# Laying the PSUM slots of 512 columns ahead of those of 1024 at the seam between retention and attention in a hybrid decoder block

## The chip, the cores and the metric

The kernel runs on one core of one Trainium2 chip. The metric is the device time of one execution in microseconds (us). The profile and the trace come from one further execution under the hardware profiler. Engines are named as the profile names them: PE (TensorE matmul), PEld (its weight loads, which overlap PE), DVE (VectorE), ACT (ScalarE), POOL (GpSimd) and SP (SyncE, which here only issues transfers).

## The reference, cut to what matters

A decoder block on 1024 tokens of width 1024 in float32: a token mixer with two parallel branches, then a squared-ReLU MLP, each behind an RMS norm with modulation. The change sits where the first branch of the mixer (retention) ends and the second (dilated attention) begins.

```python
proj = h @ w_in
rq, rk, rv, rg = parts[0], parts[1], parts[2], parts[3]
ro = retention(rq, rk, heads(rv, RET_HEADS))          # 4 heads, chunks of 128 tokens
mu = jnp.mean(ro, axis=-1, keepdims=True)
var = jnp.mean(jnp.square(ro - mu), axis=-1, keepdims=True)
ro = (ro - mu) * lax.rsqrt(var + GN_EPS)              # per token and head
ret_out = (jax.nn.silu(rg) * (ro * gn_g + gn_b)) @ w_ret_out
...
for gi, (win, dil) in enumerate(ATT_GROUPS):          # 3 groups of 4 heads
    aq, ak, av = parts[4 + 3 * gi], parts[5 + 3 * gi], parts[6 + 3 * gi]
    o, lse = dilated_group(...)                       # scores, softmax, product with the values
...
merged = sigmoid(gate_a) * ret_out + sigmoid(gate_b) * att_out
```

## The kernel before

All products are made of three passes of PE with operands split into a high and a low part (`mm3`, lines 206 to 214: low weight, low operand, then high by high). Everything is written in one fixed order; each engine takes its instructions in that order, and waits on semaphores where a tile that it needs is not written yet, or where the tile it is about to overwrite is not yet read.

**The steps around the seam.** The retention runs as 32 steps, `chunk(h, c, ...)` for 4 heads of 8 chunks (line 717). In each, PE makes the chunk's output `o` (line 761 on). DVE takes its mean and variance (`bn`, `ba`, lines 777 to 779), POOL turns them into a scale and a shift (`gr`, lines 780 to 782), ACT applies them and so moves `o` out of PSUM into `onm` (line 790). The transposition of `onm` is left to the next step: `on_T` (line 675) has PE write four 128x128 transposes into a tile `oT` (line 682), and ACT copies them out (line 686). A step also spreads some products of the gate `rg` over its idle places (`rg_mm`); ACT reads those at line 709. The last chunk, number 31, has its `on_T` in the first step of the attention.

That step is `att_step(0, 0)` (line 1848). It makes `ak`, the projection that gives the keys of one head of group 1, as eight rounds (`proj_gen`) of six 128x512 matmuls: each round has two for each of the three passes, one per half of 1024 tokens. After four rounds stands `on_T` of the last chunk; then the other four. Behind them DVE multiplies the transposed outputs with the gate (`u_final`, line 693), POOL stores them to `y`, and ACT and DVE split `ak` into `kh` and `kl` (lines 1560 and 1561). The weights of this product are the tiles `raw_7785h` (ACT, line 200) and `raw_7785l` (DVE, line 201); those of the next product, which is the second step's `ak`, are `raw_7973h` and `raw_7973l`.

**PSUM.** It holds eight banks of 512 float32 columns per partition. A pool of PSUM slots is opened for each stage by `banks` (line 154) and closed by the next one. The tags take their banks in the order in which the stage first asks for them:

- retention, `banks(False, True)` at line 1438: a slot `s` is asked for first (line 1439), so that the 5 slots `s` of one bank are banks 0 to 4 and the 3 slots `rg` are banks 5 to 7;
- attention, `banks(False)` at line 1852: the 2 slots `mm` of two banks (`ps_mm`, 1024 columns) and the 4 slots `s` of one bank (`ps_s`, 512 columns); before, `ps_mm` asks first, at line 1853;
- retention's output product, `banks(True)` at line 2192: 8 slots `s`; its accumulators are `roc` (banks 4 to 1) and `roa` (banks 0, 7, 6 and 5, in this order).

A tile of a new pool waits until the tiles of the old pool that lay in its banks have been read. In the program before, the tiles lie so: the last chunk's `o` in bank 1, its predecessor's `oT` in bank 2; the first `ak` in banks 0 and 1, the second `ak` in banks 2 and 3, and the last chunk's `oT` in bank 4. Later, in the attention's output product `ao` (slots `mm`), the last two tiles lie in banks 0 and 1 and in banks 2 and 3; DVE reads them at line 2056.

**Transfers.** SP issues the loads of weights and spilled projections through a ring of three tiles (`raw`, line 85), each as soon as DVE is through with the tile's last use. The attention's bias comes at line 1529 (`bias`), spilled keys of group 2 at line 85 (`raw<-akd`). POOL issues the stores of `y` and, two per projection, sums in DRAM (`yt`, lines 575 and 577).

## Time and profile before

| what | us |
|---|---|
| median of 3 runs | 2169.19 |
| lowest and highest of them | 2168.49, 2170.26 |
| the profiled execution's own time | 2170.22 |
| its span in the profile | 2168.4 |
| PE busy in the span | 2143.3 (99%) |
| DVE, ACT, POOL busy | 1491.4, 983.1, 203.7 |

The profiled execution took 1.03 us more than the median of the runs, and its span is 1.82 us shorter than its own time. Times within the span are counted from its start. A row of the timeline gives start, duration, engine, line, operation, output and inputs, shape and count; in square brackets stands how long the engine was idle before, and what ended that idle time. A row of the waits gives the waiting instruction, what it waited for, the total in us, how often, and the longest. Matmuls overlap, so the distance between their starts (some 0.227 us at 512 columns) is shorter than the duration that a row shows (0.39 us).

### The profile page before, as it was taken

To read this page: it belongs to the slowest core of one execution; us is meant where nothing else is said; L and a number is where in the kernel's file an instruction comes from. 1 tells how busy PE (TensorE), PEld (TensorE's weight loads), DVE (VectorE), ACT (ScalarE), POOL (GpSimd) and SP (SyncE) were. 2 spreads that over 40 slices of the span, in tenths; PEclk is the share of its full clock that TensorE was granted. 3 is DMA by queue.
4 is the path that set the end of the run, shared out by engine and by line. 5 is a ranking of instruction groups with operands and counts; after the bars stand their busy time and mean duration, and the time that the engine had idled before them with its cause. 6 is when DMAs were issued, how large, how long until landed. Compare 5 with 4: busy or idle time off the path is not lost. (4 is left out here: it accounts for less than half of the span.)

```text
span 2168.4 us, 27396 instructions
## 1 busy us (share of the span) xinstructions
PE 2143.3 (99%) x10036; PEld 1784.0 (82%) x10036; DVE 1491.4 (69%) x2320; ACT 983.1 (45%) x1769; POOL 203.7 (9%) x267
## 2 busy tenths in 40 slices
PE   8999999999999999999999999999999999999998
PEld 6888888888888888888888888888778888888887
DVE  5886777777654677665667644677876665977855
ACT  5543322323344566664756635334454455533413
POOL 0001111100001243321010000001000000000003
PEclk9999999999999999999999999999999999999999
DMA  9859998845576655537877366653244435645322
GB/s 381 282 207 305 296 293 243 232 157 200 194 289 242 228 187 179 177 120 197 209 192 202 125 241 220 217 179 131 68 170 160 151 144 195 250 130 175 107 88 78
DMA packets 162931, 425.19 MB, mean 196 GB/s; under 512 B 28261, under 2 KB 56172, under 8 KB 159724
## 3 DMA queue, kind: packets, MB, share of 16 engines
q1 hardware_dynamic: 150456, 374.90, 49.0%
q0 software_dynamic: 9648, 48.24, 10.3%
q8 instruction: 79, 1.29, 0.2%
q10 hardware_dynamic: 2692, 0.30, 0.1%
q14 instruction: 56, 0.46, 0.1%
HBM read 324.13 MB, written 160.32 MB: 223 GB/s over the span
## 5 line engine op out<-in xcount | busy, mean ns | idle before, releaser
L212 PE MATMUL qap<-hl,qaw 128*128 128x512 f32 x264 | 102.7, 389 | 0.0
L214 PE MATMUL qap<-hh,qaw 128*128 128x512 f32 x264 | 102.7, 389 | 0.0
L210 PE MATMUL qap<-hh,qaw 128*128 128x512 f32 x264 | 102.7, 389 | 0.0
L620 POOL TENSOR_TENSOR j<-qk,j 128x512 fp32r<-128x512 f32 x32 | 42.8, 1336 | 399.6 <-ACT j L619 383.8
L2256 POOL TENSOR_TENSOR accnf<-accnf,sqnf 128x256 f32<-128x256 f32 (+1 forms) x18 | 16.6, 920 | 609.6 <-ACT sqnf L2252 609.6
L2360 ACT ACTIVATE a<-a 128x512 f32<-128x512 f32 x48 | 30.3, 632 | 73.7 <-DVE a L2359 73.7
L212 PEld LDWEIGHTS qap<-hl,qaw 128*128 128x128 f32 x264 | 49.6, 188 | 10.4
L210 PEld LDWEIGHTS qap<-hh,qaw 128*128 128x128 f32 x264 | 49.6, 188 | 10.3
L214 PEld LDWEIGHTS qap<-hh,qaw 128*128 128x128 f32 x264 | 49.5, 188 | 10.3
L2568 ACT CAST w2h<-w2s 128x512 fp32r<-128x512 f32 x36 | 22.4, 621 | 78.5 <-DVE w2s L2606 74.5
L686 ACT ACTIVATE on<-oT,gnt 128x128 f32<-128x128 f32 x128 | 48.1, 455 | 19.1 <-PE oT L682 18.9
L267 DVE TENSOR_TENSOR fw<-w1r,fw 128x512 fp32r<-128x512 f32 x48 | 32.8, 688 | 33.5 <-ACT fw L257 33.5
L267 DVE TENSOR_TENSOR qaw<-wa,qaw 128x512 fp32r<-128x512 f32 x66 | 44.0, 685 | 9.4 <-ACT qaw L257 9.4
L2091 DVE TENSOR_TENSOR rwl<-rwl,rwh 128x1024 fp32r<-128x1024 f32 x25 | 30.2, 1220 | 29.1 <-ACT rwh L2121 29.1
L210 PE MATMUL fp<-h2h,fw 128*128 128x512 f32 x128 | 50.0, 391 | 0.0
L214 PE MATMUL fp<-h2h,fw 128*128 128x512 f32 x128 | 49.8, 389 | 0.0
L212 PE MATMUL fp<-h2l,fw 128*128 128x512 f32 x128 | 49.8, 389 | 0.0
L214 PE MATMUL roa<-rh,rwh 128*128 128x512 f32 x128 | 49.8, 389 | 0.0
L210 PE MATMUL roa<-rh,rwl 128*128 128x512 f32 x128 | 49.8, 389 | 0.0
L212 PE MATMUL roa<-rl,rwh 128*128 128x512 f32 x128 | 49.8, 389 | 0.0
L1620 ACT ACTIVATE P<-P,ng 128x128 f32<-128x128 f32 (+1 forms) x96 | 41.9, 439 | 16.6 <-DVE ng L1612 16.5
L656 DVE TENSOR_TENSOR sm<-sm,sT 128x128 f32<-128x128 f32 x32 | 9.2, 288 | 54.7 <-ACT sm L655 54.7
(3092 smaller groups left out, 7216.8 us busy)
## 6 DMA issues: line engine op xcount, KB each, us to landing
v<-vd SPq DMA_DIRECT2D x32, 512.0 KB, 5.4
w1r<-in_w_ff_dram SPq DMA_DIRECT2D x32, 512.0 KB, 4.6
yt<-y POOLq DMA_DIRECT2D x24, 512.0 KB, 7.9
xsd<-as SPq DMA_DIRECT2D x24, 512.0 KB, 2.8
w2r<-in_w_ff2s_dram SPq DMA_DIRECT2D x24, 512.0 KB, 7.1
cossin<-in_w_ada_dram SPq DMA_DIRECT2D x22, 512.0 KB, 3.5
em<-in_w_ada_dram SPq DMA_DIRECT2D x16, 512.0 KB, 10.2
wrvs<-in_w_rv_dram POOLq DMA_DIRECT2D x16, 512.0 KB, 9.9
```

The costliest lines, as they stand in the source:

```text
L210: nc.tensor.matmul(o, wl, xh, start=first, stop=False, skip_group_check=skip)
L212: nc.tensor.matmul(o, wh, xl, start=False, stop=False, skip_group_check=skip)
L214: nc.tensor.matmul(o, wh, xh, start=False, stop=last, skip_group_check=skip)
L267: nc.vector.tensor_sub(t[:, 512:], src, fv(t[:, :512]))
L620: nc.gpsimd.tensor_sub(t[:, 1], src, fv(t[:, 0]))
L656: nc.vector.tensor_add(sm, sm, ps[:, C:2 * C])
L686: nc.scalar.activation(hd["on", h, c // 4][e][:, c % 4 * C:(c % 4 + 1) * C], po[:, e, :], AF.Identity, scale=gnv[0][:, neg + i:neg + i + 1 ...
L1620: nc.scalar.activation(v, v, AF.Exp, bias=ng[:, blk:blk + 1], accum_out=st[:, g, blk, 2 + a:3 + a])
L2091: nc.vector.tensor_sub(lo, fv(lo), fv(hi))
L2256: (nc.vector if f == 7 else nc.gpsimd).tensor_add(G["acc", key], G["acc", key], sq)
L2360: nc.scalar.activation(o, o, AF.Relu)
L2568: nc.scalar.copy(hi, src)
```

## The change

```diff
     def on_T(h, c):
 
-        po = ps_s(f"oT{h}{c}", (P, 4, P))
+        po = (hd.pop("oT", None) or ps_s(f"oT{h}{c}")).rearrange("p (a b) -> p a b", a=4)
         on = hd["o", h, c]
...
             if pair == a == 0:
                 banks(False)
+                hd["oT"] = ps_s("oT")
             ps = ps_mm(f"ak{pair}1{a}")
```

The tile for the last chunk's transposes is asked for ahead of the first `ak`, and `on_T` takes it when it comes. So the 4 slots `s` of the attention are banks 0 to 3, and its 2 slots `mm` banks 4 to 7. The other calls of `on_T` get the same tile as before, in another notation. Lines behind 1852 stand one further down in the changed file; line numbers in this document are those of before unless it says so. No instruction of any engine is added, dropped or moved; what changes is where PSUM tiles of the attention lie, and with it what the first users of a bank wait for. The first `ak` now lies in bank 4, where the `oT` of chunk 29 lay, and bank 5, where a tile of the last gate product but one lay; the second `ak` in banks 6 and 7, over the two tiles of the last gate product; the last `oT` in bank 0, over the `o` of chunk 30. The last `ao` tiles lie in banks 4 and 5 and in banks 6 and 7.

PE's order with its waits, at the first `ak` (`o_8465` is the last chunk's output, `oT_8475` the transposes of the chunk before it, `hh` and `hl` the normed input), before:

```order
L214 MATMUL o_8465<-v_8162,smh_8383 128x512
L682 MATMUL oT_8475<-ct,onm_8428 128x128 [waits Activation_49]
L682 MATMUL oT_8475<-ct,onm_8428 128x128 x3
L210 MATMUL ak_8501<-hh_86,raw_7785l 128x512 [waits Activation_49]
L210 MATMUL ak_8501<-hh_86,raw_7785l 128x512
L212 MATMUL ak_8501<-hl_94,raw_7785h 128x512 x2
```

and now:

```order
L214 MATMUL o_8465<-v_8162,smh_8383 128x512
L682 MATMUL oT_8475<-ct,onm_8428 128x128 [waits Activation_49]
L682 MATMUL oT_8475<-ct,onm_8428 128x128 x3
L210 MATMUL ak_8502<-hh_86,raw_7785l 128x512 [waits DVE_49]
L210 MATMUL ak_8502<-hh_86,raw_7785l 128x512
L212 MATMUL ak_8502<-hl_94,raw_7785h 128x512 [waits Activation_49]
```

The wait of before is for ACT's line 790 of the last chunk, which reads `o_8465` out of bank 1. Now the first matmul waits for DVE's line 201 that writes its own weight `raw_7785l`, and the third for ACT's line 200 that writes `raw_7785h`; nothing of the product waits for a reader of a bank any more.

Four rounds further on PE comes to the last chunk's transposes, `oT`, which now carry a wait of their own (rows of the changed program):

```order
L214 MATMUL ak_8502<-hh_89,raw_7785h 128x512 x2
L682 MATMUL oT<-ct,onm_8495 128x128 [waits Activation_49]
L682 MATMUL oT<-ct,onm_8495 128x128 x3
L210 MATMUL ak_8502<-hh_90,raw_7785l 128x512 x2
L212 MATMUL ak_8502<-hl_98,raw_7785h 128x512 x2
```

It is the wait for ACT's line 790 of the last chunk, whose result `onm_8495` they transpose; before, the product ahead of them had waited for the same instruction already, and they carried none. It has moved behind 24 matmuls.

The other place is PE's seam between the attention's output product and retention's, some 300 us later (`roa_11384` is the first accumulator there, in bank 0, `roa_11399` the second, in bank 7). The pieces of the difference:

```order
-L210 MATMUL roa_11384<-rh_11168,rwl_11118 128x512 [waits DVE_49,Activation_49]
+L210 MATMUL roa_11384<-rh_11168,rwl_11118 128x512 [waits Activation_49]
 L212 MATMUL roa_11384<-rl_11110,rwh_11244 128x512 [waits Activation_49]
 L214 MATMUL roa_11384<-rh_11168,rwh_11244 128x512
...
-L210 MATMUL roa_11399<-rh_11168,rwl_11118 128x512
+L210 MATMUL roa_11399<-rh_11168,rwl_11118 128x512 [waits DVE_49]
 L212 MATMUL roa_11399<-rl_11110,rwh_11244 128x512
 L214 MATMUL roa_11399<-rh_11168,rwh_11244 128x512
```

Before, the first accumulator waited for DVE's reading of the last `ao` tile but one, which had lain in bank 0. Now the second accumulator, 12 matmuls later, waits for DVE's reading of the very last `ao` tile, which had lain in banks 6 and 7. Otherwise one wait of PE on itself is gone from the second `ak` and one from the accumulator `roc` in bank 3; the orders of DVE, ACT, POOL and SP and their waits are the same as before.

## The prediction

> **What bounds the kernel.** I read the page first, then PE's waits, then the timeline around the changed place.

> ```profile
> span 2168.4 us, 27396 instructions
> PE 2143.3 (99%) x10036; PEld 1784.0 (82%) x10036; DVE 1491.4 (69%) x2320; ACT 983.1 (45%) x1769; POOL 203.7 (9%) x267
> ```

> PE is busy for 2143.3 of 2168.4 us, so at most 25.1 us can be won without taking work from it. What a change of waits is worth is read from the list of PE's own waits, here its first three rows:

> ```profile
> engine line waited for: us in total, times, longest us
> PE pb L444 <- DMA onehot<-in_onehot_dram: 5.6, 2, 4.3
> PE ak L210 <- ACT onm L790: 3.0, 1, 3.0
> PE fp L212 <- DVE xt L2398: 2.0, 2, 1.1
> ```

> The second row is the place of the change: once, the projection `ak` stood 3.0 us for ACT's line 790. No longer stall is in the list but the load at the start of the program. PE's timeline shows it from both sides:

> ```profile
> 974.06 0.60 PE L682 MATMUL oT<-ct,onm 128*128 128x128 f32 x4
> 977.69 0.73 PE L210 MATMUL ak<-hh,raw_7785l 128*128 128x512 f32 x2 [3.04 <-ACT onm L790]
> 978.26 0.62 PE L212 MATMUL ak<-hl,raw_7785h 128*128 128x512 f32 x2
> ...
> 983.28 0.60 PE L682 MATMUL oT<-ct,onm 128*128 128x128 f32 x4
> 983.63 0.71 PE L210 MATMUL ak<-hh,raw_7785l 128*128 128x512 f32 x2
> 984.18 0.62 PE L212 MATMUL ak<-hl,raw_7785h 128*128 128x512 f32 x2
> ```

> Both times four transposes stand ahead of the same kind of matmul. At 983.28 the product goes on 0.35 us after the first transpose began; at 974.06 it takes 3.63 us. Why, the other engines' rows between them show:

> ```profile
> 974.26 0.70 DVE L777 BATCH_NORM_STATS2 bn<-o 128x6 f32<-128x512 f32 x1 [3.74 <-PE o L214]
> ...
> 975.38 0.19 POOL L780 TENSOR_TENSOR gr<-ba,ct 128x1 f32<-128x1 f32 x1 [7.87 <-DVE ba L778]
> 975.64 0.92 POOL L781 TENSOR_TENSOR gr<-gr,ct 128x1 f32<-128x1 f32 x1
> 976.64 0.19 POOL L782 TENSOR_TENSOR gr<-gr 128x1 f32<-128x1 f32 x1
> 976.86 0.78 ACT L790 ACTIVATE onm<-o,gr 128x512 f32<-128x512 f32 x1 [0.67 <-POOL gr L782]
> ```

> The last chunk's `o` passes through DVE, POOL and ACT before ACT has read it out of bank 1, at 976.86 + 0.78 = 977.64; 0.05 us later PE starts `ak`, which lies in that bank. `ak` needs none of that chain's values: it is a wait for a place.

> **The change part by part.** No instruction is added or dropped, on any engine; what counts is which waits end last.

> (1) The wait for line 790 leaves the first `ak`. What takes its place are waits for the weights and, for the next product, the banks of the gate:

> ```profile
> 969.29 1.23 DVE L201 TENSOR_TENSOR raw_7785l<-raw,raw_7785h 128x1024 fp32r<-128x1024 f32 x1 [1.85 <-ACT raw_7785h L200]
> 971.98 1.08 ACT L709 ACTIVATE srg<-rg 128x512 f32<-128x512 f32 x2 [2.72 <-PE rg L214]
> ```

> The low weight is there at 970.52 and the high one, which it is made from, by 969.29, some 4 us ahead of need. The two tiles of the last gate product, under the second `ak`, are read by 973.06; the other two tiles under the first `ak` were read earlier. So PE goes on as it does at 983.28: 3.63 - 0.35 = 3.28 us won, and another 0.02 since the first two matmuls there are 0.55 us apart from the third, not 0.57. **3.30 us.** The bounds are the 3.04 us of recorded idle time below and 3.30 above; I take 3.30, since the row at 983.28 is the same sequence without the wait.

> (2) The last chunk's transposes now wait for line 790 themselves. They stand 5.59 us behind the start of `ak` (983.28 - 977.69), so they come at 983.28 - 3.30 = 979.98, and `onm` is there at 977.64: 2.34 us to spare, no cost. Were that cover gone, PE and all that is queued behind the transposes would wait by what is missing.

> (3) While `ak` now runs from 974.41, ACT and DVE still read `oT` and `o` from banks 2 and 1. The same overlap is in the trace: ACT's 1.50 us of copies out of `oT` beside `ak`,

> ```profile
> 983.91 1.50 ACT L686 ACTIVATE on<-oT,gnt 128x128 f32<-128x128 f32 x4 [5.34 <-PE oT L682]
> 984.40 4.30 DVE L693 TENSOR_TENSOR on<-on,srg 128x512 f32<-128x512 f32 x7 [3.97 <-ACT on L686]
> ```

> where `ak` keeps its pace (0.62 us for a pair, at 984.18 as at 978.26). Cost 0. These rows also show that the followers move along: ACT waits for the transposes, DVE for ACT; POOL's stores of `y` and SP's later loads wait for DVE. They come 3.30 us earlier with PE.

> (4) At the seam some 300 us later, the second accumulator `roa` now waits until DVE has read the last `ao`:

> ```profile
> 1282.69 0.39 PE L210 MATMUL roa<-rh,rwl 128*128 128x512 f32 x1
> ...
> 1282.89 1.22 DVE L2056 TENSOR_TENSOR g<-g,ao 128x1024 f32<-128x1024 f32 x1 [4.22 <-PE ao L214]
> ...
> 1285.41 0.39 PE L210 MATMUL roa<-rh,rwl 128*128 128x512 f32 x1
> ```

> The 13th matmul of `roa` starts at 1285.41, and the reading ends at 1282.89 + 1.22 = 1284.11. DVE was idle for 4.22 us before it, waiting for PE, so it keeps this distance: 1.30 us to spare, cost 0. If DVE were late by more than that, PE would wait for the excess, with ACT and DVE behind it; that needs a second thing to be late, and nothing in the change makes one. The wait that leaves the first `roa` cost nothing either: there is no row for it in PE's waits.

> The sum against the profiled execution: 3.30 us, so the span goes from 2168.4 to 2165.1 and its own time from 2170.22 to 2166.9. That execution stands 1.03 us over the median of the runs; for the median, 2169.19 - 3.30 = **2165.9 us**.

> **Does it last to the end?** Later waits of PE (such as the row with `fp`) are for DVE and ACT working on PE's own results, and move along. Only transfers could keep their old times. This is the place with the least room:

> ```profile
> 1003.13 1.01 ACT L1560 CAST kh<-ak 128x1024 fp32r<-128x1024 f32 x1 [10.82 <-PE ak L214]
> ...
> 1009.62 0.32 SPq L85 DMA_DIRECT2D raw<-akd  x1
> ...
> 1019.01 1.05 ACT L1551 CAST kh<-raw 128x1024 fp32r<-128x1024 f32 x1 [6.03 <-DMA raw<-akd]
> ...
> 1019.08 0.51 POOL L577 DMA_DIRECT2D yt<-yt  x1 [9.41 <-DMA yt<-y]
> ...
> 1020.10 1.23 DVE L1552 TENSOR_TENSOR kl<-raw,kh 128x1024 fp32r<-128x1024 f32 x1 [3.73 <-ACT kh L1551]
> ...
> 1022.21 0.28 PE L212 MATMUL sc<-kl,qh 128*128 128x128 f32 x1
> ```

> The keys of group 2 land 9.39 us after SP's issue, `kl` is ready at 1021.33, and PE wants it at 1022.21: 0.88 us to spare. The issue itself follows DVE's work behind `kh` at 1003.13, which waits for PE, so it moves along too.

> **The rivals.**

> A. Transfers keep their times. If those keys land at 1019.01 as before, `kl` is ready at 1021.33, where PE now wants it at 1022.21 - 3.30 = 1018.91: a new stall of 2.42 us, and 0.88 us is left of the gain: 2168.3. For it speaks that the load runs in a crowded stretch, as the window of its ten us shows:

> ```profile
> 1010.00:1020.00 10.00, 10.00 (x64) 8.88 (x63) 5.74 (x8) 3.97 (x10) 0.51 (x1) 1.00 0.86 240
> ```

> The last but one number is the mean busy share of the DMA engines, 0.86. Against it: `kh` at 1003.13 ended a wait of 10.82 us for PE, so the issue follows PE, and the transfers beside it follow the stores of `y`, which follow PE too. [...]

> B. Slower. The issue order at the same place changes: the earlier load falls behind one more whole `yt` transfer of POOL, 9.41 us by its row. It would be issued at 1006.32, land 18.80 us later at 1025.12, and `kl` be ready another 2.32 us on (1021.33 - 1019.01) at 1027.44: a stall of 8.53 us against 1018.91, net 5.23 us slower: 2174.4. It decides from a landing of 9.39 + 0.88 + 3.30 = 13.57 us after the issue. Against it: POOL's `yt` sums follow the stores of `y`, which move by the same 3.30 us, and one `yt` transfer already ran beside this load.

> C. The change does not remove the wait: PE starts `ak` at 977.69 for another reason. Then the time stays at 2169.2. Against it: nothing else that `ak` waits for ends after 970.52.

> **How the numbers follow.** Forecast 2165.9 with 0.84; A 0.07, B 0.05, C 0.04. A measurement of this kernel can tell from no change about 0.2%, which is 4.34 us: 3.30 us lies within it. The fastest run of before is 0.70 us under the median, the slowest 1.07 over, so the forecast may read 2164.8 to 2167.0, and a reading below 2164.85 has some 0.08, from the forecast's tail. Slower holds B's 0.05; the rest, 0.87, is within 0.2%. The range reaches from 2164.0 (the forecast less 1.07 for the scatter of the runs and 0.8, a quarter of the gain, for what I may have sized too small) to 2169.4 (A with 1.07 more, which takes in C); it leaves out B.

> **What would show it.** In the changed kernel's profile, PE's list has no row of `ak` on line 790, the first `ak` matmul stands 0.35 us behind the transposes (at 974.41), the last transposes follow 5.57 us later without idle time, and no row of `roa` on DVE's line of `ao` (one line further down now) appears. A shows as a new row of `sc` waiting for `kl`, with 2 us or so; B as the same row with more than 3.3. The prediction is wrong if the gain in the span is under 2 or over 4.3 us.

## The result, and the profile after

The changed kernel took 2165.70 us, the median of 22 runs (2164.59 to 2172.95). The kernel before, on the same chip, took 2170.15 us, also the median of 22 runs (2168.07 to 2175.38). The ratio is 0.9979, with a 95% interval of 0.9972 to 0.9985: 4.5 us won, and by the interval between 3.3 and 6.1 us. The predicted 2165.9 us is within 0.2 us of the measured time, but partly by luck. The gain was not the predicted 3.30 us but 1.2 us more, and the three runs that the prediction started from lay 1.0 us under the median of the 22.

The profiled execution of the changed kernel took 2165.45 us. Its span and engine totals:

```profile
span 2163.6 us, 27394 instructions
PE 2141.4 (99%) x10036; PEld 1782.8 (82%) x10036; DVE 1492.1 (69%) x2320; ACT 983.5 (45%) x1769; POOL 203.2 (9%) x267
```

The span is 4.8 us shorter than before. All engines carry out as many instructions as before; the two fewer in the total are semaphore waits. PE's waits in the changed kernel, the first rows:

```profile
engine line waited for: us in total, times, longest us
PE pb L444 <- DMA onehot<-in_onehot_dram: 5.6, 2, 4.3
PE fp L212 <- DVE xt L2399: 2.0, 2, 1.0
PE av L876 <- ACT hh L413: 1.7, 1, 1.7
```

The row of `ak` on line 790 is gone, and no new row has come in its place: neither `oT` nor `roa` nor `sc` waits for anything. PE's timeline at the seam (start, duration, engine, line, operation, tiles), changed kernel:

```profile
972.56 0.60 PE L682 MATMUL oT<-ct,onm 128*128 128x128 f32 x4
972.91 0.71 PE L210 MATMUL ak<-hh,raw_7785l 128*128 128x512 f32 x2
973.46 0.63 PE L212 MATMUL ak<-hl,raw_7785h 128*128 128x512 f32 x2
...
978.50 0.60 PE L682 MATMUL oT<-ct,onm 128*128 128x128 f32 x4
978.85 0.71 PE L210 MATMUL ak<-hh,raw_7785l 128*128 128x512 f32 x2
```

The first `ak` follows 0.35 us behind the transposes, where it took 3.63 us before, and the last transposes come 5.59 us later without idle time. That is the picture the prediction drew. From the first of these transposes to the end of the span it is 2163.6 - 972.56 = 1191.0 us, and before 2168.4 - 974.06 = 1194.3 us: behind the seam **3.3 us** are won, as forecast. The other 1.5 us of this pair of profiles lie ahead of the seam, where the two programs are the same. Most of that is at the very start: some forty matmuls in, the same one starts at 22.11 us before and at 21.21 now, 0.9 us apart. It begins in the eight matmuls from 15 us on. In the kernel before:

```profile
15.04 3.13 PE L876 MATMUL av<-wv0wh,hl 128*128 128x512 f32 x8
```

and in the changed one:

```profile
14.81 2.01 PE L876 MATMUL av<-wv0wh,hl 128*128 128x512 f32 x8
```

The same eight matmuls took 3.13 us in one execution and 2.01 in the other. In 14 profiles of this study the first transposes of the seam stand anywhere from 972.12 to 974.19 us, kernels of before and of the change mixed. So this part is scatter of the executions, and the spans of two single profiles can't settle a gain of 3 us. What the medians show beyond 3.3 us is another matter, and most experiments went to that.

### The profile page after: what moved, and what is told of

It is laid out like the page before. It is cut to its first block, busy times and chain, and to the rows that moved or that the text cites. A ratio compares the mean times of both kernels' runs of the same rounds, so it can differ in the third digit from the quotient of the medians.

```text
span 2163.6 us, 27394 instructions
## 1 busy us (share of the span) xinstructions
PE 2141.4 (99%) x10036; PEld 1782.8 (82%) x10036; DVE 1492.1 (69%) x2320; ACT 983.5 (45%) x1769; POOL 203.2 (9%) x267
## 3 DMA queue, kind: packets, MB, share of 16 engines
q8 instruction: 79, 1.29, 0.2%
## 5 line engine op out<-in xcount | busy, mean ns | idle before, releaser
L210 PE MATMUL qap<-hh,qaw 128*128 128x512 f32 x264 | 102.7, 389 | 0.0
L212 PE MATMUL qap<-hl,qaw 128*128 128x512 f32 x264 | 102.7, 389 | 0.0
L214 PE MATMUL qap<-hh,qaw 128*128 128x512 f32 x264 | 102.7, 389 | 0.0
L214 PEld LDWEIGHTS qap<-hh,qaw 128*128 128x128 f32 x264 | 49.6, 188 | 10.4
L212 PEld LDWEIGHTS qap<-hl,qaw 128*128 128x128 f32 x264 | 49.5, 188 | 10.3
L210 PEld LDWEIGHTS qap<-hh,qaw 128*128 128x128 f32 x264 | 49.5, 188 | 10.3
L686 ACT ACTIVATE on<-oT,gnt 128x128 f32<-128x128 f32 x128 | 48.2, 455 | 15.7 <-PE oT L682 15.6
L210 PE MATMUL fp<-h2h,fw 128*128 128x512 f32 x128 | 50.0, 390 | 0.0
L212 PE MATMUL fp<-h2l,fw 128*128 128x512 f32 x128 | 49.8, 389 | 0.0
L214 PE MATMUL fp<-h2h,fw 128*128 128x512 f32 x128 | 49.8, 389 | 0.0
L210 PE MATMUL roa<-rh,rwl 128*128 128x512 f32 x128 | 49.8, 389 | 0.0
L212 PE MATMUL roa<-rl,rwh 128*128 128x512 f32 x128 | 49.8, 389 | 0.0
L214 PE MATMUL roa<-rh,rwh 128*128 128x512 f32 x128 | 49.8, 389 | 0.0
```

Source lines behind the costliest of these rows:

```text
L210: nc.tensor.matmul(o, wl, xh, start=first, stop=False, skip_group_check=skip)
L212: nc.tensor.matmul(o, wh, xl, start=False, stop=False, skip_group_check=skip)
L214: nc.tensor.matmul(o, wh, xh, start=False, stop=last, skip_group_check=skip)
L686: nc.scalar.activation(hd["on", h, c // 4][e][:, c % 4 * C:(c % 4 + 1) * C], po[:, e, :], AF.Identity, scale=gnv[0][:, neg + i:neg + i + 1 ...
```

## The experiments

**The theories.** S: the change takes away 3.3 us of waiting at the seam, these pass to the end one for one, and nothing else happens; what the medians show beyond it is scatter. K: PE's long idle stretch costs more than its length, because in part of the executions the granted TensorE clock falls behind it; a change that removes the stretch wins that too. L: moved code, and not the PSUM layout, makes the difference. "To the end" below is the time from the seam's first transposes to the end of the span; it leaves out the scatter ahead of the seam.

### Controls, and a first clock drop

`ctl_same` is the kernel before with an empty statement, so that only line numbers move; `chg_again` is the changed kernel with one.

```diff
                 banks(False)
+                pass
```

> The kernel before, with one empty statement more. Seam theory (the change is worth the 3.28 us between the transposes and the first ak, and nothing else): ratio 1.000, the gap from the start of the four transposes to the first ak 3.6 us as before, from those transposes to the end of the span 1194.3 us within 0.5; the time from the span's start to them may differ by 1 to 2 us between two executions of one program. Rival (the changed program is also faster ahead of the seam, 4.5 us in all): here too ratio 1.000, but the start of those transposes at 974.06 within 0.3 us, since the program is the same.

> The changed kernel, with one empty statement more. Seam theory: 3.3 us faster than before, ratio 0.9985, transposes to end of span 1191.0 us within 0.5, and the transposes may start anywhere between 972 and 975. Rival (also faster ahead of the seam): ratio 0.9979 again, 4.5 us, and the transposes start at 972.6 within 0.3 us again.

The control took 2171.32 us against 2171.25 (ratio 1.0000, 0.9991 to 1.0009). The changed kernel again took 2165.87 against the same runs: ratio 0.9976 (0.9967 to 0.9984), 5.2 us won, and 1191.0 us to the end as forecast. Its transposes start at 972.79, which would also fit the rival of a program that is faster ahead of the seam. Against that rival stand `ctl_look`, the program of before with them at 972.22, and `late_change`, a changed program with them at 974.19 (both below). An empty statement moves no instruction, so these two controls do not test L. It falls by runs further down that do add instructions and keep the time to the end within 0.4 us: `late_change` has 1190.6 us against 1191.0 of the change, `fill_before` 1194.0 against 1194.3 of before. What was not expected stands in the control's own profile. PE's timeline at the seam:

```profile
973.69 0.60 PE L682 MATMUL oT<-ct,onm 128*128 128x128 f32 x4
977.33 0.72 PE L210 MATMUL ak<-hh,raw_7785l 128*128 128x512 f32 x2 [3.04 <-ACT onm L790]
...
978.36 0.66 PE L214 MATMUL ak<-hh,raw_7785h 128*128 128x512 f32 x2
978.82 1.05 PE L210 MATMUL ak<-hh,raw_7785l 128*128 128x512 f32 x2
...
981.38 1.01 PE L210 MATMUL ak<-hh,raw_7785l 128*128 128x512 f32 x2
982.23 0.62 PE L212 MATMUL ak<-hl,raw_7785h 128*128 128x512 f32 x2
```

The wait is the same as in the profile of before, 3.04 us. But from 978.82 on a pair of matmuls takes 1.05 us, not 0.62, and four pairs later it is 0.62 again. The starts of these pairs lie 0.85 us apart, where others lie 0.455: 4 x 0.40 = 1.6 us lost on top of the wait. The windows of the same kernel, 3.41 us each, show why (the last three numbers of a row are the granted clock, the DMA share and GB/s):

```profile
975.39:978.80 3.41, 1.47 (x6) 1.24 (x7) 0.96 (x2) 2.15 (x4) 1.00 (x2) 1.00 0.23 82
978.80:982.21 3.41, 3.41 (x9) 2.63 (x8) 1.27 (x2) 0.00 (x0) 0.60 (x1) 0.50 0.46 135
982.21:985.62 3.41, 3.41 (x18) 2.82 (x17) 0.00 (x0) 0.44 (x2) 0.00 (x0) 1.00 0.24 96
```

For 3.41 us the clock was granted at 0.50, and the view has 9 records of matmuls there against 18 in the window behind it. PE's busy time is no guide to it: it reads 3.41 in both. This profile had one further stall in its list of PE's waits that before's does not have:

```profile
PE gate L210 <- DVE raw_8961l L201: 2.4, 1, 2.4
```

The weight is late because of a transfer, but not its own. DVE and ACT make it behind the softmax weights, and for those DVE waited for statistics that come back from DRAM (`stn`):

```profile
1056.11 0.18 DVE L1701 TENSOR_TENSOR mx<-mx,stn 128x16 f32<-128x16 f32 x1 [3.37 <-DMA stn<-std]
```

In the profile of before DVE did not wait there. To the end the control took 1198.3 us, which is 1194.3 + 1.6 + 2.4; the 1194.3 us that were forecast for it were missed by these two.

A second control is `ctl_look`, the kernel before with two empty statements:

> The kernel before with two empty statements more: one more look at whether the granted clock falls behind the 3.04 us. Clock theory: either 1.00 throughout and the last transposes 5.59 us behind the first ak, or below 0.7 in a window of 4 us behind it and the distance longer by 1.3 us or more. Rival: always 1.00 and 5.59 us.

```profile
971.28:974.69 3.41, 1.54 (x9) 1.06 (x7) 1.69 (x4) 1.51 (x4) 1.07 (x2) 1.00 0.09 35
974.69:978.10 3.41, 2.24 (x10) 1.86 (x11) 1.32 (x2) 1.72 (x2) 0.23 (x2) 1.00 0.22 82
978.10:981.51 3.41, 3.41 (x17) 2.77 (x16) 0.51 (x1) 0.00 (x0) 0.60 (x1) 1.00 0.68 228
```

It took 2168.39 us, and here, as in the profile of before, the clock stays at 1.00 (to the end: 1194.4 us). The wait is in every profile of this kernel; the drop is not.

### The layout alone: `half_layout`

The tile is asked for ahead but used by nobody; `on_T` stays as before.

```diff
                 banks(False)
+                ps_s("ahead")
```

> A slot of 512 columns is asked for ahead and never used, and the transposes take their own slot as before: the layout of the change without the hand-over of its tile. Seam theory: the same as the change, gap 0.35 us and 1191.0 us from the transposes to the end. Rival (the hand-over matters): anything else, up to 1194.3.

It took 2166.48 us, and 1191.6 us to the end, with 0.7 us of a gate stall in it. The first `ak` stands at 973.42, 0.36 us behind the transposes at 973.06. So the order in which the stage asks for its slots is the whole change, and handing the tile over to `on_T` does nothing for the time.

### The dose at the seam: `bank2s` and `bank2`

In both the first `ak` is moved from banks 0 and 1 to banks 2 and 3, by a slot that is asked for ahead of it and in which DVE sets one column to zero. It then waits for ACT's reading of the `oT` of chunk 30 (line 686), which ends some 1.4 us before line 790. `bank2s` also tries to put the later tiles back as they were:

```diff
                 banks(False)
+                nc.vector.memset(ps_mm("ahead")[:, 0, 0:1], 0.0)
...
+            if j == 0:
+                nc.vector.memset(ps_mm("ahead2")[:, 0, 0:1], 0.0)
```

> Half the dose: the layout of before, but the first ak in banks 2 and 3, over the oT of chunk 30, which ACT reads until 1.50 us after it starts at 974.70 (so until 976.20), and not over the last o (until 977.64). A second such touch ahead of the output product sets its tiles back to the banks of before. Seam theory: the first ak waits for ACT's line 686 for 1.6 us of recorded idle time instead of 3.0, the gap from the transposes to it is 2.2 us instead of 3.63, and 1.4 us are won to the end (1192.9 us from the transposes). Rival (the gain is in the layout of the whole attention, not in this wait): no gain, 1194.3.

At the seam it did what was meant, but elsewhere it did harm. Its waits of PE:

```profile
PE ao L210 <- ACT g L2004: 3.3, 1, 3.3
...
PE ak L210 <- ACT on L686: 1.6, 1, 1.6
```

My second line put the first `ao` over a slot that ACT was still reading: 3.3 us of waiting there, where it had been 0.7. And behind that wait the clock dropped as well, in the windows of the same kernel:

```profile
1238.13:1241.54 3.41, 1.29 (x6) 1.07 (x7) 1.82 (x5) 2.90 (x3) 0.00 (x0) 1.00 0.64 190
1241.54:1244.95 3.41, 3.41 (x10) 2.63 (x9) 0.91 (x2) 0.00 (x0) 0.00 (x0) 0.50 0.94 321
```

So its 2172.90 us (ratio 1.0007, 0.9998 to 1.0015) says nothing on the dose. `bank2` is the same kernel without the second edit. It has the same amount of waiting as before, but in two pieces: 1.6 us at the seam, and 1.4 us at `roa`, since the `ao` tiles change banks.

> The first ak in banks 2 and 3, over the oT of chunk 30, and nothing set back behind it, so that retention's first accumulator lies over the last ao: idle 1.6 us at the first seam and 1.4 us at the second, together the 3.0 us of before, but in two pieces. Clock theory: no lower clock behind either piece, and so 1 to 3 us below before in the median, with little spread. Rival (idle time adds up, in pieces or in one): ratio 1.000.

```profile
PE ak L210 <- ACT on L686: 1.6, 1, 1.6
PE roa L210 <- DVE g L2057: 1.4, 1, 1.4
```

It took 2169.33 us (2168.11 to 2171.80), ratio 0.9991 (0.9982 to 0.9999): with 3.0 us of waiting as before, slightly faster than before. In its windows the clock is 1.00 at both places.

### The same seam elsewhere: `seam_before`

The kernel before with the second line of `bank2s` alone. Its `ao` tiles change banks, so that the first `roa` waits for the reading of the very last `ao`, without the 1.30 us to spare that the change has.

```diff
+            if j == 0:
+                nc.vector.memset(ps_mm("ahead2")[:, 0, 0:1], 0.0)
```

> The kernel before, with the tiles of the output product ao in each other's banks, so that retention's first accumulator in bank 0 lies over the last ao and not over the last but one. Seam theory by the prediction's step 4: PE waits at the first roa until DVE has read that ao, 1284.11 in the trace of before, where it went on at 1282.69; so a new row of roa on line 2056 (a few lines further down here) of some 1.3 us idle time, 1.4 us lost, 1195.7 us from the transposes to the end. Rival (a place's last reader costs nothing when PE is 99% busy): no row, 1194.3.

```profile
PE ao L210 <- ACT g L2003: 3.3, 1, 3.3
PE ak L210 <- ACT onm L790: 3.0, 1, 3.0
...
PE roa L210 <- DVE g L2058: 1.4, 1, 1.4
```

The wait at `roa` came as forecast from the rows, 1.41 us against 1.3. Again `ao` waited 3.3 us by a side effect of the edit. The clock fell to 0.50 at both long waits, for 3.41 us behind that of `ak` and for 6.82 us from 1.2 us ahead of the end of that of `ao` on, and it was 1.00 behind the short one at `roa`, in every window from 1280 to 1300 us:

```profile
977.27:980.68 3.41, 3.41 (x10) 2.67 (x9) 1.23 (x2) 0.00 (x0) 0.60 (x1) 0.50 0.50 149
...
1240.10:1243.51 3.41, 2.21 (x5) 1.82 (x6) 2.66 (x5) 2.08 (x3) 0.00 (x0) 0.50 0.93 305
1243.51:1246.92 3.41, 3.41 (x9) 2.65 (x9) 0.00 (x0) 0.00 (x0) 0.00 (x0) 0.50 0.88 291
```

It took 2177.74 us in its one run, against 2170.19 for before, and 1203.8 us to the end, not the 1195.7 that were forecast without the wait at `ao` and the drops.

### A later line 790: `late_before`, `late_change`, `late_change5`, `late_change7`

ACT's line 790 of the last chunk is carried out 2, 6 or 8 times with the same result. In the kernel before this makes `ak` wait longer; in the changed one it eats the 2.34 us that step (2) found to spare at the last transposes.

```diff
-        nc.scalar.activation(on, po, AF.Identity, scale=gr[:, 1:2], bias=gr[:, 2:3])
+        for _ in range(2 if g == NG - 1 else 1):
+            nc.scalar.activation(on, po, AF.Identity, scale=gr[:, 1:2], bias=gr[:, 2:3])
```

> The kernel before; ACT does the last chunk's line 790 twice, the second time with the same result, which ends it 0.68 us later. Seam theory: the first ak waits 0.68 us longer, 3.7 us of idle time, gap 4.3 us, and the end comes 0.7 us later: 1195.0 us from the transposes to the end. Rival: unchanged at 3.0 us, for something else ends the wait.

> The changed kernel; ACT does the last chunk's line 790 twice, 0.68 us later. Seam theory: nothing waits for it before the last transposes, which have 2.34 us to spare: no row, 1191.0 us from the transposes to the end. Rival (the wait has only moved to another place): 0.7 us lost.

A repeat costs 0.81 us (two took 1.59 us, one 0.78), not the 0.68 that I had taken, an estimate of mine that no run shows. In the kernel before, PE's list has `ak` waiting 3.9 us, and the run took 2174.81 us, 4.6 more than before beside it. Not all of that is the clock's: the longer wait is 0.8 us of it, and the gate's weight was late here too, by 1.9 us, behind another wait of DVE for `stn`. Two windows of 3.41 us in a row were at 0.50:

```profile
973.55:976.96 3.41, 0.29 (x3) 0.06 (x1) 1.59 (x4) 2.37 (x6) 1.31 (x3) 1.00 0.20 77
976.96:980.37 3.41, 2.67 (x6) 2.15 (x7) 1.75 (x2) 1.63 (x2) 0.00 (x0) 0.50 0.02 5
980.37:983.78 3.41, 3.41 (x9) 2.64 (x8) 0.08 (x1) 0.00 (x0) 0.60 (x1) 0.50 0.71 231
```

In the changed kernel the same edit costs nothing: 2166.60 us, no row in PE's waits, 1190.6 us to the end. ACT is through at 978.59 and the last transposes stand at 980.13.

> The changed kernel; ACT does the last chunk's line 790 six times, which ends it 5 x 0.68 = 3.40 us later. Seam theory: that is 1.06 us more than the transposes' 2.34 us to spare; a row of oT on line 790 of some 1.1 us, 1.1 us lost (1192.1 us from the transposes to the end). Rival (the transposes have other cover, or none): no row, or 3.4 us lost.

Now the spare time is used up. `late_change5`, PE's timeline:

```profile
981.65 0.66 PE L682 MATMUL oT<-ct,onm 128*128 128x128 f32 x4 [1.61 <-ACT onm L791]
```

Five repeats are 4.06 us, less 2.35 to spare: 1.71 us; the transposes came 1.76 us late, and it took 1193.05 us to the end, 2.0 more than the changed kernel. The clock stayed at 1.00. The time of the single run was 2168.75 us.

> The changed kernel; ACT does the last chunk's line 790 eight times, which ends it 7 x 0.78 = 5.46 us later and lets the last transposes wait 5.46 - 2.34 = 3.1 us: the idle stretch of before, put back at another place and for another tile. Clock theory: 3.1 us slower than the change plus the lower clock in a part of the runs, so 4 to 5 us in the median, and the wider spread of before; ratio to before about 1.000. Rival (only the wait itself counts, 3.1 us): 0.9991 of before if the change alone is 0.9977.

With seven repeats the idle stretch is as long as the one that the change removes, but it stands 24 matmuls later:

```profile
982.95 0.66 PE L682 MATMUL oT<-ct,onm 128*128 128x128 f32 x4 [3.24 <-ACT onm L791]
```

It took 2171.24 us (2168.33 to 2176.13), ratio to before 1.0003 (0.9994 to 1.0012). The changed kernel had a ratio of 0.9976 against the runs of before beside it: 3.24 us of idle time cost some 5.9 us by the two ratios, whose intervals together leave room for 2 to 10 us. In the execution that was profiled the clock was 1.00 in every window from 962 to 994 us.

### The same wait, filled: `fill_before`

While the first `ak` of the kernel before waits, PE carries out 13 matmuls of 512 columns into a free slot. Their sums are read by nobody; everything else is computed as before. The slot that they take moves the later tiles of 512 columns by one slot.

```diff
             ps = ps_mm(f"ak{pair}1{a}")
+            if pair == a == 0:
+                fill = ps_s("fill")
+                w = args[-1]
+                for _ in range(13):
+                    nc.tensor.matmul(fill, w[0][:, :P], hx[0][0][0], start=True, stop=True)
```

> The kernel before, but PE runs 13 matmuls of 512 columns, whose sums nobody reads, while the first ak waits for line 790: 13 x 0.227 = 2.95 us of work in the 3.04 us. Clock theory (the idle stretch costs its 3.3 us, and in a part of the executions a lower granted clock behind it, 1.3 us and more each time): ak still starts 3.6 us behind the transposes, but PE's idle time is some 0.1 us, the granted clock is 1.00 in the 12 us behind it, and the time is 1 to 3 us below before (ratio 0.9990 or so), with runs that lie closer together. Rival (the change gains more than 3.3 us for another reason): ratio 1.000, same spread as before.

```profile
973.11 0.60 PE L682 MATMUL oT<-ct,onm 128*128 128x128 f32 x4
973.47 3.24 PE L1858 MATMUL fill<-hh,raw_7785h 128*128 128x512 f32 x13
976.76 0.74 PE L210 MATMUL ak<-hh,raw_7785l 128*128 128x512 f32 x2
```

The `ak` starts 3.65 us behind the transposes, as before, and PE has 0.05 us of idle time there. It took 2169.62 us, ratio 0.9995 (0.9986 to 1.0004). The time alone leaves it open, since the interval holds both no gain and the 1.7 us that K wants by the next section.

### The granted clock over all runs

What the times of `fill_before` leave open, the granted clock does not. Each run lists its mean, to a thousandth. One window of 3.41 us at 0.50 takes 0.5 x 3.41 / 2170 = 0.0008 off that mean, so single runs can't be told apart, but means over runs can: by the scatter of the runs they are good to some 0.0002. In the windows of the profiles the clock falls in two kinds of place: at the end of stretches in which PE has been idle for 3.04 us or more, or behind them, and at the end of the program, where it is 0.50 for the last 7.4 us in the profile of before and for the last 5.6 us in that of the change. The second kind takes 0.0017 and 0.0013 off the means of these two, which is about the 0.0015 that even the change lacks. The waits in the second column are those of PE at the seam, at `ao` or at `roa`:

| kernel | long waits of PE | runs | mean granted clock | median us | ratio to before |
|---|---|---|---|---|---|
| the change | none | 22 | 0.99845 | 2165.70 | 0.9979 |
| `chg_again` | none | 12 | 0.99850 | 2165.87 | 0.9976 |
| `fill_before` | 3.0 filled with matmuls | 11 | 0.99845 | 2169.62 | 0.9995 |
| `bank2` | 1.6 and 1.4 | 11 | 0.99845 | 2169.33 | 0.9991 |
| before, beside `ctl_same` | 3.0 | 29 | 0.99766 | 2171.25 | 1 |
| before, beside `bank2` | 3.0 | 29 | 0.99766 | 2170.71 | 1 |
| `ctl_same` | 3.0 | 12 | 0.99767 | 2171.32 | 1.0000 |
| `late_change7` | 3.2, at `oT` | 12 | 0.99792 | 2171.24 | 1.0003 |
| `bank2s` | 1.6, and 3.3 at `ao` | 12 | 0.99750 | 2172.90 | 1.0007 |

The kernels fall into two groups: 0.9984 to 0.9985 without a stretch of 3 us in which PE is idle, and 0.9975 to 0.9979 with one. The difference between before and the change, 0.0008, is one window at half clock per run on average; over 2170 us it is 1.7 us. With this, S alone falls. 3.3 us for the wait and 1.7 for the clock make 5.0 us; measured were 4.5 and 5.2, by the ratios. `fill_before` and `bank2` keep the 3.3 us and lose the clock's part: by the ratios they lie 4.1 and 3.3 us over `chg_again`, which ran on another chip, and they lie 1.1 and 1.4 us under the runs of before beside them.

## Why the prediction was right, and where it was wrong

- **Step (1), the wait leaves the first `ak`: the place is right.** The 0.35 us between the transposes and `ak` is as forecast, and the stretch from the seam to the end is 3.3 us shorter. The lowest times of the two kernels, 2164.59 and 2168.07, also differ by 3.5 us.
- **The sum, 3.30 us, was mis-sized.** It priced the idle stretch at its own length. Measured were 4.5 us (3.3 to 6.1) and, once more, 5.2 us (3.5 to 7.2). The missing term is the granted clock behind the stretch, 1.7 us by the mean clock. The prediction's rows could not show it, since the profiled execution of before had no drop at the seam; the step that the clock stays as it was had not been thought of at all. The bound "3.30 above" was therefore no bound. Nor is the 25.1 us of time without PE a ceiling for what can be won, since PE reads as busy through a window at half clock (3.41 of 3.41 us in `ctl_same`). The measured change, 0.21%, lies just outside the 0.2% that had been given 0.87 (its interval reaches from 0.15% to 0.28%).
- **Step (2), the last transposes wait for line 790 with 2.34 us to spare: right.** In the changed kernel:

```profile
975.37 0.78 ACT L790 ACTIVATE onm<-o,gr 128x512 f32<-128x512 f32 x1 [0.67 <-POOL gr L782]
```

ACT is through at 976.15, the transposes stand at 978.50: 2.35 us. `late_change` and `late_change5` bracket it, one repeat free and five costing 1.76.
- **Step (3), no cost from ACT's and DVE's readings beside `ak`: right.** The second pair of `ak` takes 0.63 us in the rows above, where it took 0.62 before.
- **Step (4), `roa` waits for DVE's reading of the last `ao` with 1.30 us to spare: right.** Rows of the changed kernel, first `roa`, DVE's reading, 13th `roa`:

```profile
1277.93 0.39 PE L210 MATMUL roa<-rh,rwl 128*128 128x512 f32 x1
...
1278.13 1.22 DVE L2057 TENSOR_TENSOR g<-g,ao 128x1024 f32<-128x1024 f32 x1 [4.22 <-PE ao L214]
...
1280.65 0.39 PE L210 MATMUL roa<-rh,rwl 128*128 128x512 f32 x1
```

1280.65 - (1278.13 + 1.22) = 1.30 us. Where this distance is missing, in `seam_before` and `bank2`, PE does wait, by 1.4 us.
- **"Does it last to the end", and rivals A and B: the forecast was right, its margin was not.** Rows of the changed kernel on the keys of group 2:

```profile
1004.84 0.84 SPq L85 DMA_DIRECT2D raw<-akd  x1
...
1009.95 1.05 ACT L1551 CAST kh<-raw 128x1024 fp32r<-128x1024 f32 x1 [0.23 <-DMA raw<-akd]
...
1011.51 1.22 DVE L1552 TENSOR_TENSOR kl<-raw,kh 128x1024 fp32r<-128x1024 f32 x1
...
1017.43 0.28 PE L212 MATMUL sc<-kl,qh 128*128 128x128 f32 x1
```

The issue came 4.78 us earlier, as far as PE (the first `roa`, some 260 us later, still starts 4.76 us earlier), and the landing not later but still earlier: 5.11 us behind the issue, not 9.39. So `kl` is ready at 1012.73 with 4.70 us to spare, where it was 0.88. Neither the landing time nor the span of the load is fixed here, in one pair of profiles; A, which wanted the landing to stay, didn't occur.
- **"Wrong if the gain in the span is under 2 or over 4.3 us."** The gain was 4.8 us, so by this mark it was wrong. But 1.5 us of it lie ahead of the seam and are scatter of the two executions; behind it were 3.3. A mark on the span was badly chosen; it should have stood on the stretch from the seam to the end.

**What stays open** is which idle stretch brings the drop. Of eight stretches of 3.0 us or more behind the program's start, five were followed by one (`ctl_same`, `late_before`, `seam_before` twice, `bank2s` at `ao`) and three not (before, `ctl_look`, `late_change7`). PE's busy share of the window ahead doesn't decide it alone: a window with 1.47 us busy came ahead of the drop in `ctl_same`, and one with 1.47 us in the profile of before was followed by none:

```profile
973.19:976.60 3.41, 1.47 (x9) 1.02 (x7) 1.69 (x4) 1.50 (x4) 1.11 (x2) 1.00 0.08 30
```

Ahead of all five drops stood a window with at most 1.51 us of busy PE; without a drop the emptiest windows had 1.47, 1.54 (`ctl_look`) and 1.76 us (`late_change7`, whose 3.24 us of idle time stand in two windows, with 1.76 and 1.83 us of busy PE). No run set on purpose where the stretch lies against the windows, so whether that plays a part is not shown. The late weight of the gate stood behind DVE's wait for `stn` in all three profiles that have it (`ctl_same` 2.4, `late_before` 1.9, `half_layout` 0.7 us). It came and went with executions of the same program, and no run tried to remove it.

## What to carry to other kernels

When a stage opens new PSUM slots, choose the order of asking so that its first tiles fall on the banks that were read longest ago: the order sets who waits for whom (here `ak` came 3.63 us behind the transposes in one order and 0.35 in the other), and a wait for a place can be moved under work that has time to spare (here 2.35 us). Price an idle stretch of TensorE like the one here at more than its length: 3.04 us of it were worth 4.5 and 5.2 us. And look at the granted clock behind it in several profiles, not in one: it was 0.50 for 3.41 us in `ctl_same`, and 1.00 in the profile of before. To compare single profiles, count from the changed place to the end, not the whole span.

## What the runs showed of the hardware that was not expected

The idle time that was followed by a drop, and that which was not, lie close together. 3.04 us of recorded idle time, 3.64 us counted from the start of the four transposes ahead of it, was enough in `ctl_same` and in `seam_before`, and not in the profile of before. Windows with 1.29 to 1.51 us of busy PE, and in `late_before` one with 0.29 us, came directly ahead of a drop. 1.6 us of idle time in three profiles (`bank2s`, `bank2`, `late_change5`) were followed by none, and behind the 2.4 us at the gate in `ctl_same` a pair of matmuls took 0.62 us, as at full clock.
